# Eight weight buffers instead of six, x^T at two places in its tiles, early side loads on the main queue

## The chip, the cores and the metric

The kernel runs on one core of a Trainium2 chip, in one launch. The metric is device microseconds (us) of that core. The parts of the core that matter are TensorE (matrix products, PE in the rows; its weight loads are listed apart as PEld), VectorE (DVE), ScalarE (ACT), GpSimd (POOL) and SyncE (SP). SP computes nothing here: its sequence issues the loads, and an issue whose buffer is not free yet waits there with all that stand behind it. GpSimd's sequence issues loads too, among its own small operations.

## The reference

Two layers over 512 tokens of width 1024, in fp32. Layer 0 mixes the tokens by retention (4 heads), layer 1 by dilated sliding-window attention (3 groups of 16 heads, with a relative-position bias); behind each mixer stands a SwiGLU FFN of inner width 2816, and each of the four parts ends in a residual sum and a layer norm.

```
for i in range(2):
    mix = retention(x, w_in, w_out) if i == 0 else dilated_attention(x, w_in, w_out, rel_bias)
    x = layer_norm(1.414 * x + mix, gain[i, 0], bias[i, 0])
    gate, up = split(x @ w_up[i])
    x = layer_norm(1.414 * x + (silu(gate) * up) @ w_down[i], gain[i, 1], bias[i, 1])
```

In the retention, per head, the scores are q k^T times a decay table, y is the scores times v, normalised per token, and z = silu(gate) * y is multiplied by the output weights. In the attention the exponentials of the three groups share one maximum, are summed, divided once, and go through the output weights.

## The kernel before, in words

**Numbers.** Every fp32 operand of a large product is split into two parts, hi and lo, of a rounder fp32 type, and a product is three matmuls into the same accumulator, hi hi, hi lo, lo hi (`mm3`, line 278). In a trace row of a matmul the operand that moves is named first and the stationary one (brought by a weight load) second: in `bank<-xhi,whi 128x512` 512 columns of x^T move over 128 x 128 of a weight. x^T lies in `xhi` and `xlo` as 8 tiles of 128 features by 512 tokens. In the gates and in the q and k projections x^T moves over weights; in v, in the down projections (h) and in the output projections (z) the weights move over x^T, h or z.

**Weights.** All weights come in units of 128 x 1024 floats (512 KB), in an order fixed in advance (`plan`). A unit is loaded into one of six raw buffers (`wraw`, lines 66 to 80, on SP), split on ScalarE (`whi`, line 133) and on VectorE (`wlo`, line 134), two units ahead of its use. `load` issues the next load when the unit six places before it has been read by its last reader (lines 68 and 69). The first four units are loaded in halves, with the pieces of x^T between them.

**FFN.** The up projection goes through quads: four weight blocks n to n+3 against four quarters of x^T, in seven products instead of eight. The seven parts of a quad, each 24 matmuls of 256 columns, are in order block n, block n+1, a difference (n minus a sum), T1 against n+2, and so on (`up_rest`, line 773); the moving operands are quarters of x^T or combinations of them (T1 to T4). Three of the seven weight operands are sums of blocks, made on VectorE (`make_sum`, line 97, the instructions of line 107). The first of them needs n+2 plus n+3: block n+3 is loaded a second time, by GpSimd, and added into the raw buffer of n+2 in the transfer itself (`add_blocks`, line 89). A part that adds into a bank that has been in use waits until ScalarE has copied the bank (`copied`, line 739). Quads come in chunks of 4, 4 and 3; behind each chunk stand its down projections (8, 8 and 6 units, each 24 matmuls of 512 columns). In the first chunk of each FFN the work is mixed with the layer norm's last steps; the four later ones follow one pattern.

**Placement in SBUF.** Pools are laid out one behind the other in the order of their opening: constants, x^T and the residual, the raw buffers, a pad of 80 floats, the split weights, a small pool for statistics, and then the pools of the stage (retention, FFN, attention).

**Start.** SP first loads weights and x^T, then cosines, sines and the following units. GpSimd's sequence loads the columns for the layer norm (`cols`), the bias table and its one-hot matrices (`rbT`, `onehot`, both into the residual's tiles `r`, which are free then) and the decay tables (`dec`). TensorE uses the one-hot matrices in `bias_rows`, between the projections of q, k and v of the first head; the result is written to memory (`rows_dram`), from where GpSimd loads bias tables (`tab`, lines 882 and 889) for each pair of heads in the attention. For the powers in the norms GpSimd has one small operation per block of tokens (`rstd`, line 324: `grs` in the retention, `rs` in the layer norms).

Of the kernel before, what the change touches and what calls it, by code (L numbers as in the profile page):

```python
# [7 lines left out]
F32 = mybir.dt.float32  # L8
F32R = mybir.dt.float32r
# [6 lines left out]
P = 128  # L16
D = 1024
T = 512
KT = D // P
# [5 lines left out]
HD = 64  # L25
# [10 lines left out]
W0, W1, W2 = (2 * RES - 1) * PH, 256, 256  # L36
WB = W0 + W1 + W2
S0 = 7 * P


class Weights:
# [107 lines left out]
def trunk(tc, a, out):  # L149
    nc = tc.nc  # L150
    plan = []

    def ret_plan(h):
        qk = [(a["w_rqk"], 4 * h + i) for i in range(4)]
        v = [(a["w_rv"], 4 * h + i) for i in range(4)]
        g = [(a["w_rg"], 4 * h + i) for i in range(4)]
        o = [(a["w_ro"], 4 * h + i) for i in range(4)]
        return qk, v, g, o

    def ffn_plan(i):  # L160
        q = 0
        for n in FC:
            todo = [(q + k, j) for k in range(n) for j in range(7)]
            if q == 0:
                todo.sort(key=lambda t: (t[1] if t[0] < 2 and t[1] < 2 else 2))
                todo[4:9] = [(0, j) for j in (5, 3, 2, 6, 4)]
            plan.extend((a[f"w_up{i}"], 4 * k, j) for k, j in todo)
            plan.extend((a[f"w_dn{i}"], 2 * q + j) for j in range(2 * n))
            q += n

    rp = [ret_plan(h) for h in range(RH)]
    plan += rp[0][0] + rp[0][1]
    for h in range(RH):
        plan += rp[h][2]
        if h + 1 < RH:
            plan += rp[h + 1][0] + rp[h + 1][1]
        plan += rp[h][3]
    ffn_plan(0)
    tiles = {
        "qk": lambda p, i: [(a["w_aqk"], 6 * p + i)],  # L180
        "v": lambda q, g: [(a["w_av"], 6 * q + 2 * g + i) for i in range(2 + 2 * g)],
        "o": lambda q, _: [(a["w_ao"], 2 * q + i) for i in range(2)],
    }
    first, steps = att_schedule()
    for kind, *at in first + [s for t in steps for s in t]:
        if kind in tiles:
            plan += tiles[kind](*at)
    plan += tiles["o"](3, 0)
    ffn_plan(1)

    with tc.tile_pool(name="const", bufs=1) as cpool, tc.tile_pool(
        name="xpool", bufs=1
    ) as xpool, tc.tile_pool(name="wraw", bufs=6) as wraw, tc.tile_pool(
        name="pad", bufs=1
    ) as pad, tc.tile_pool(name="whl", bufs=4) as whl, tc.tile_pool(name="lnp", bufs=2) as lnp, tc.tile_pool(
        name="ps", bufs=8, space=PSUM
    ) as ps, tc.tile_pool(name="scratch", bufs=1, space=DRAM) as dr:
        pad.tile([P, 80], F32, name="pad")
        ws = Weights(nc, plan, wraw, whl, 2, 6)
        c = Core(nc, tc, a, out, ws, cpool, xpool, lnp, ps, dr)  # L200
        c.retention()
        c.ffn(0)
        c.attention(first, steps)
        c.ffn(1)
# [43 lines left out]
class Core:  # L248
    def __init__(self, nc, tc, a, out, ws, cpool, xpool, lnp, ps, dr):
        self.nc, self.tc, self.a, self.out, self.ws = nc, tc, a, out, ws  # L250
        self.lnp, self.ps, self.dr = lnp, ps, dr
        self.xhi = xpool.tile([P, KT, T], F32R, name="xhi")
        self.xlo = xpool.tile([P, KT, T], F32R, name="xlo")
        self.xw = [xpool.tile([P, 2, T], F32, name=f"xw{i}") for i in range(2)]
        self.r = [xpool.tile([P, D], F32, name=f"r{b}") for b in range(NB)]
        self.ident = cpool.tile([P, P], F32, name="ident")
        make_identity(nc, self.ident)
        self.mhalf = cpool.tile([P, 1], F32, name="mhalf")
        nc.vector.memset(self.mhalf, -0.5)
        self.cols = cpool.tile([P, 2, 2, KT], F32, name="cols")  # L260
        nc.gpsimd.dma_start(out=self.cols, in_=a["ln_cols"])
        self.on_read = False
        self.pending = []
        self.halves = False

    def bank(self):
        return self.ps.tile([P, T], F32, name="bank")
# [64 lines left out]
    def next_halves(self, i):  # L332


        self.halves, self.of = True, i

    def finish(self, b):
        for t, op in ((self.gain, ALU.mult), (self.bias, ALU.add)):
# [163 lines left out]
    def retention(self):  # L502
        nc, tc, a = self.nc, self.tc, self.a
        with tc.tile_pool(name="rt", bufs=1) as rt:
            self.rt = rt
            self.cos = rt.tile([P, T], F32, name="cos")
            self.sin = rt.tile([P, T], F32, name="sin")
            self.warm_up(rt)
            self.load_x(rt)
            nc.sync.dma_start(out=self.cos, in_=a["cos"])  # L510
            nc.sync.dma_start(out=self.sin, in_=a["sin"])
            qk = self.ret_qk()
            self.bias_rows()
            v = self.ret_v()
            for b in range(NB):
                nc.sync.dma_start(out=self.r[b], in_=a["x"][b * P : (b + 1) * P, :])
            self.next_halves(0)
            for h in range(RH):
                s = self.ret_scores(h, qk)
                g = [None] * 4  # L520
                last = h == RH - 1
                if not last:
                    for e in range(4):
                        g[e] = self.ret_gate(e)
                    y = self.ret_y(s, v)
                    qk = self.ret_qk()
                    tr = self.ret_transpose(y)
                    z = self.ret_z(g, tr)
                    v = self.ret_v()
                    self.rows_product(z, h == 0, False)  # L530
                else:
                    for e in range(2):
                        g[e] = self.ret_gate(e)
                    y = self.ret_y(s, v)
                    g[2] = self.ret_gate(2)
                    tr = self.ret_transpose(y)
                    g[3] = self.ret_gate(3)
                    z = self.ret_z(g, tr)
                    self.rows_product(z, False, True)

    def warm_up(self, rt):
# [78 lines left out]
    def ret_scores(self, h, qk):  # L620
        nc, rt = self.nc, self.rt
        dec = rt.tile([P, T], F32, name="dec", bufs=2)
        nc.gpsimd.dma_start(out=dec, in_=self.a["decay"][h])
        q, k = qk
        s = []
        for J in range(NB):
            n = T - J * P
            bk = self.bank()
            for d in range(2):
                self.mm3(  # L630
                    bk[:, :n],
                    (k[d][0][:, J * P : (J + 1) * P], k[d][1][:, J * P : (J + 1) * P]),
                    (q[d][0][:, J * P :], q[d][1][:, J * P :]),
                    d == 0,
                    d == 1,
                )
            t = rt.tile([P, T], F32, name="stmp", bufs=2)
            nc.vector.tensor_tensor(out=t[:, :n], in0=bk[:, :n], in1=dec[:, :n], op=ALU.mult)
            hi = rt.tile([P, n], F32R, name=f"s{J}hi")
            lo = rt.tile([P, n], F32R, name=f"s{J}lo")  # L640
            self.split(hi, lo, t[:, :n])
            s.append((hi, lo))
        return s
# [52 lines left out]
    def ffn(self, i):  # L696
        nc, tc = self.nc, self.tc
        with tc.tile_pool(name=f"ff{i}", bufs=1) as ff:
# [5 lines left out]
            self.xs = {"B11": self.x_block(0, 0), "B21": self.x_block(1, 0), "B22": self.x_block(1, 1)}  # L704
            self.xs["T1"] = self.x_block(0, 1)
            self.x_late = {}
            for n in ("T2", "T3", "T4"):
                self.xs[n] = [ff.tile([P, 4, T // 2], F32R, name=f"{n}{p}") for p in ("hi", "lo")]
            for ch, n in enumerate(FC):
                if ch == 1:  # L710
                    self.ln_params(2 * i + 1, *params)
# [6 lines left out]
                zs = [(hi[:, j, :], lo[:, j, :]) for hi, lo in quads for j in range(2)]  # L718
                last = ch == len(FC) - 1
                self.halves = False  # L720
                self.rows_product(zs, ch == 0, last, final=last and i == 1, finish=ch == 0)
    def part(self, bank, x, start=False):

# [97 lines left out]
    def attention(self, first, steps):  # L821
        nc, tc = self.nc, self.tc
        with tc.tile_pool(name="at", bufs=1) as at:
# [3 lines left out]
            self.vt += [at.tile([P, 12, P], F32, name=f"v{i}") for i in (1, 2)]  # L827
            self.ones = at.tile([P, P], F32R, name="ones")
            nc.vector.memset(self.ones.bitcast(F32), 1.0)
            self.half = at.tile([P, HD], F32, name="half")  # L830
            nc.vector.memset(self.half, 1.0)
            self.qt, self.kt = (
                [[at.tile([P, T], F32R, name=f"{w}{i}{n}") for n in ("hi", "lo")] for i in range(NG)]
                for w in "qk"
# [2 lines left out]
            n = 4  # L837
# [10 lines left out]
    def bias_rows(self):  # L848

        nc = self.nc  # L850
# [1 line left out]
        oh1 = self.r[2][0:33, 0 : W1 + W2]  # L852
        rows0, rows1 = self.r[1][0:AH, 0:W0], self.r[0][0:AH, 0 : W1 + W2]
        nc.gpsimd.memset(rb[32:33, :], NEG)
        nc.gpsimd.dma_start(out=rb[0:32, :], in_=self.a["rbT"])
        nc.gpsimd.dma_start(out=oh0, in_=self.a["onehot"][:, 0:W0])
        nc.gpsimd.dma_start(out=oh1, in_=self.a["onehot"][:, W0:WB])
        half = W0 // 2
        parts = [(0, oh0[:, :half], rows0[:, :half]), (0, oh0[:, half:], rows0[:, half:])]
        parts += [(1, oh1[:, :W1], rows1[:, :W1]), (2, oh1[:, W1:], rows1[:, W1:])]  # L860
# [220 lines left out]
    def att_pv(self, p, _):  # L1081
# [23 lines left out]
                lambda t: t[:, 2 * J * P : 2 * J * P + n], False, J == 3,  # L1105
            )
        for h in range(2):
            self.mm(den[h * HD : (h + 1) * HD], self.half, e[:, h], True, True)
        self.pv = bk, den, e

    def att_norm(self, p, _):
# [136 lines left out]
```

## Time and profile before

| what | us |
|---|---|
| median of 3 runs (lowest to highest) | 1703.7 (1700.6 to 1705.23) |
| the profiled execution | 1714.11 |
| its span, first to last instruction | 1712.3 |
| TensorE busy | 1654.3 (97%) |
| VectorE busy | 1067.7 (62%) |
| ScalarE busy | 648.4 (38%) |
| GpSimd busy | 220.5 (13%) |

The mean granted clock of TensorE is 0.982 of full speed over the span. Busy times say how long an engine had an instruction in work, and a matmul at a lower clock is busy for longer; a long busy time is thus not the same as much work. The windows below give both: the busy time of a stretch and, in the column PEclk, the clock in it.

### The profile page before, as it was taken

What the parts mean: (1) busy time and instruction counts of PE and PEld (TensorE: products, weight loads), DVE (VectorE), ACT (ScalarE), POOL (GpSimd) and SP (SyncE); (2) the same over time, 40 slices, a digit from 0 to 9 for tenths busy, and PEclk for the clock granted to TensorE, in tenths of its full rate; (3) what the DMA queues carried; (4) which work ended last, traced back from release to release, by engine and by line L of the source; (5) the groups of instructions that cost most, each with busy time, mean ns of one, the idle gap of its engine ahead of it and who ended that gap; (6) DMA issues with size and microseconds to landing.
All of it is one profiled execution on the core that took longest, in us unless ns stands there. A gap on an engine that the chain in (4) does not pass through costs nothing. (4 is left out here: it accounts for less than half of the span.)

```text
span 1712.3 us, 24333 instructions
## 1 busy us (share of the span) xinstructions
PE 1654.3 (97%) x9972; PEld 1432.7 (84%) x9972; DVE 1067.7 (62%) x1391; ACT 648.4 (38%) x937; POOL 220.5 (13%) x307
## 2 busy tenths in 40 slices
PE   9999999999899899899999999999999899989997
PEld 6888888888898898899878788788877898888896
DVE  6454454647994674657265574567569995575565
ACT  4322232325652451444332332333233752443351
POOL 0000000000000000006232332233311000000002
PEclk9999999999999999899999999999999999999999
DMA  7322223222453433433232223223321444334321
GB/s 276 129 71 96 74 72 101 87 74 79 126 166 106 115 114 94 114 111 100 98 95 79 86 87 87 87 76 97 88 74 50 117 130 148 99 112 134 90 84 50
DMA packets 52896, 174.33 MB, mean 102 GB/s; under 512 B 7764, under 2 KB 9828, under 8 KB 52784
## 3 DMA queue, kind: packets, MB, share of 16 engines
q1 hardware_dynamic: 44272, 155.81, 27.1%
q0 software_dynamic: 8512, 16.97, 5.6%
q8 instruction: 78, 1.28, 0.3%
q14 instruction: 34, 0.28, 0.1%
HBM read 170.57 MB, written 2.17 MB: 101 GB/s over the span
## 5 line engine op out<-in xcount | busy, mean ns | idle before, releaser
L134 DVE TENSOR_TENSOR wlo<-wraw,whi 128x1024 fp32r<-128x1024 f32 (+1 forms) x278 | 339.8, 1228 | 361.2 <-ACT whi L133 360.1
L133 ACT ACTIVATE whi<-wraw 128x1024 fp32r<-128x1024 f32 (+1 forms) x278 | 292.7, 1055 | 675.3 <-PE bank L270 357.7
L270 PE MATMUL bank<-xhi,whi 128*128 128x256 f32 (+1 forms) x1376 | 459.4, 334 | 9.1 <-ACT xhi L275 8.4
L270 PE MATMUL bank<-xhi,wlo 128*128 128x256 f32 (+1 forms) x1376 | 456.3, 332 | 3.6 <-DVE wlo L134 3.6
L270 PE MATMUL bank<-xlo,whi 128*128 128x256 f32 (+1 forms) x1376 | 455.8, 331 | 1.5 <-DVE xlo L276 1.5
L270 PEld LDWEIGHTS bank<-xhi,whi 128*128 128x128 f32 x1376 | 261.3, 190 | 40.2 <-ACT xhi L275 11.4
L270 PEld LDWEIGHTS bank<-xhi,wlo 128*128 128x128 f32 x1376 | 261.4, 190 | 32.5 <-DVE wlo L134 4.8
L270 PEld LDWEIGHTS bank<-xlo,whi 128*128 128x128 f32 x1376 | 261.6, 190 | 28.3 <-DVE xlo L276 2.1
L270 PE MATMUL bank<-whi,hlo 128*128 128x512 f32 x352 | 138.7, 394 | 0.0
L270 PE MATMUL bank<-wlo,hhi 128*128 128x512 f32 x352 | 138.0, 392 | 0.0
L270 PE MATMUL bank<-whi,hhi 128*128 128x512 f32 x352 | 136.8, 389 | 0.0
L882 POOL DMA_DIRECT2D tab<-rows_dram x128 | 69.5, 552 | 198.5 <-DVE s L1006 196.1
L133 ACT ACTIVATE whi<-sum 128x1024 fp32r<-128x1024 f32 x66 | 70.1, 1063 | 62.6 <-PE bank L270 51.9
L89 POOL DMA_DIRECT2D wraw<-in_w_up_dram x22 | 19.1, 869 | 559.3 <-DMA wraw<-in_w_up_dram 276.0
L454 DVE TENSOR_TENSOR r<-r,bank 128x512 f32<-128x512 f32 x78 | 52.3, 683 | 57.3 <-PE bank L270 57.3
L270 PE MATMUL bank<-whi,xlo 128*128 128x512 f32 (+1 forms) x256 | 86.0, 336 | 0.0
L270 PE MATMUL bank<-whi,xhi 128*128 128x512 f32 (+1 forms) x256 | 86.0, 336 | 0.0
L270 PE MATMUL bank<-wlo,xhi 128*128 128x512 f32 (+1 forms) x256 | 85.7, 335 | 0.0
L134 DVE TENSOR_TENSOR wlo<-sum,whi 128x1024 fp32r<-128x1024 f32 x66 | 80.4, 1220 | 8.1 <-ACT whi L133 8.1
L270 PE MATMUL bank<-T3hi,whi 128*128 128x256 f32 x176 | 57.8, 328 | 25.6 <-ACT tmp L739 25.6
L270 PEld LDWEIGHTS bank<-wlo,hhi 128*128 128x128 f32 x352 | 66.1, 188 | 15.1
L270 PEld LDWEIGHTS bank<-whi,hhi 128*128 128x128 f32 x352 | 66.1, 188 | 14.4
(279 smaller groups left out, 3006.2 us busy)
## 6 DMA issues: line engine op xcount, KB each, us to landing
wraw<-in_w_up_dram SPq DMA_DIRECT2D x88, 512.0 KB, 3.6
wraw<-in_w_aqk_dram SPq DMA_DIRECT2D x48, 512.0 KB, 3.5
wraw<-in_w_dn_dram SPq DMA_DIRECT2D x44, 512.0 KB, 3.6
wraw<-in_w_av_dram SPq DMA_DIRECT2D x24, 512.0 KB, 3.5
wraw<-in_w_up_dram POOLq DMA_DIRECT2D x22, 512.0 KB, 6.5
wraw<-in_w_rv_dram SPq DMA_DIRECT2D x16, 512.0 KB, 4.2
wraw<-in_w_rg_dram SPq DMA_DIRECT2D x16, 512.0 KB, 4.9
wraw<-in_w_ro_dram SPq DMA_DIRECT2D x16, 512.0 KB, 3.5
```

The lines of the kernel that those rows point to most:

```text
L89: self.nc.gpsimd.dma_start(out=self.raw_tiles[u], in_=a[n + 3], accum_op=ALU.add)
L133: self.nc.scalar.activation(hi[:, c], src[:, c], AF.Copy)
L134: self.nc.vector.tensor_tensor(out=lo[:, c], in0=src[:, c], in1=hi[:, c].bitcast(F32), op=ALU.subtract)
L270: self.nc.tensor.matmul(out=out, lhsT=lhsT, rhs=rhs, start=start, stop=stop, skip_group_check=self.on_read)
L454: nc.vector.tensor_tensor(out=dst, in0=dst, in1=bk, op=ALU.add)
L882: self.nc.gpsimd.dma_start(out=tab[r * RUN : (r + 1) * RUN, h, b * P : (b + 1) * P].rearrange("p (r l) -> p r l", r=RES), in_=src(h * WB + ...
```

## The change

The raw buffers become eight (`bufs` of the pool and of `Weights`). The room comes from the memory that the kernel sets aside for the descriptors of GpSimd's transfers, `dynamic_dma_scratch_size`, which is now 8192 bytes per partition, and from one small tile of ones that another now serves for. The pool for statistics stands first behind the constants, and the pad ahead of the split weights is gone. The x^T tiles are 128 columns longer; x^T lies at their start, and from a layer norm ahead of an FFN until that FFN's down projections it lies 48 floats further (`place_x`). T2 to T4 are put behind a pad of 48 floats in the FFN's pool, with a pad of 80 behind them. The loads of `cols`, `rbT`, `onehot` and of the first two decay tables are issued on SP. The mark from which GpSimd's accumulating loads for the first FFN may be issued (`next_halves(0)`, which sets `of`) stands ahead of the last output product instead of ahead of the heads.

```diff
+SHIFT = 48
@@ trunk @@
-    ) as xpool, tc.tile_pool(name="wraw", bufs=6) as wraw, tc.tile_pool(
-        name="pad", bufs=1
-    ) as pad, tc.tile_pool(name="whl", bufs=4) as whl, tc.tile_pool(name="lnp", bufs=2) as lnp, tc.tile_pool(
+        name="lnp", bufs=2
+    ) as lnp, tc.tile_pool(name="xpool", bufs=1) as xpool, tc.tile_pool(
+        name="wraw", bufs=8
+    ) as wraw, tc.tile_pool(name="whl", bufs=4) as whl, tc.tile_pool(
-        pad.tile([P, 80], F32, name="pad")
-        ws = Weights(nc, plan, wraw, whl, 2, 6)
+        ws = Weights(nc, plan, wraw, whl, 2, 8)
@@ Core @@
-        self.xhi = xpool.tile([P, KT, T], F32R, name="xhi")
-        self.xlo = xpool.tile([P, KT, T], F32R, name="xlo")
+        self.xt = [xpool.tile([P, KT * T + P], F32R, name=n) for n in ("xhi", "xlo")]
+        self.place_x(0)
-        nc.gpsimd.dma_start(out=self.cols, in_=a["ln_cols"])
+    def place_x(self, shift):
+        self.xhi, self.xlo = [
+            t[:, shift : shift + KT * T].rearrange("p (k t) -> p k t", t=T) for t in self.xt
+        ]
@@ next_halves @@
         self.halves, self.of = True, i
+        self.place_x(SHIFT)
@@ retention @@
+            nc.sync.dma_start(out=self.cols, in_=a["ln_cols"])
-            self.next_halves(0)
...
                     z = self.ret_z(g, tr)
+                    self.next_halves(0)
                     self.rows_product(z, False, True)
@@ ret_scores @@
-        nc.gpsimd.dma_start(out=dec, in_=self.a["decay"][h])
+        (nc.sync if h < 2 else nc.gpsimd).dma_start(out=dec, in_=self.a["decay"][h])
@@ ffn @@
+            ff.tile([P, SHIFT], F32, name="pad")
             for n in ("T2", "T3", "T4"):
                 self.xs[n] = [ff.tile([P, 4, T // 2], F32R, name=f"{n}{p}") for p in ("hi", "lo")]
+            ff.tile([P, P - SHIFT], F32, name="pad2")
...
                 self.halves = False
+                self.place_x(0)
@@ attention @@
-            self.half = at.tile([P, HD], F32, name="half")
-            nc.vector.memset(self.half, 1.0)
...
-            self.mm(den[h * HD : (h + 1) * HD], self.half, e[:, h], True, True)
+            self.mm(den[h * HD : (h + 1) * HD], self.ones[:, 0:HD].bitcast(F32), e[:, h], True, True)
@@ bias_rows: rbT and the two parts of onehot @@
-        nc.gpsimd.dma_start(...)
+        nc.sync.dma_start(...)
@@ kernel @@
-    nc = bacc.Bacc("TRN2", target_bir_lowering=False, num_devices=1)
+    nc = bacc.Bacc("TRN2", target_bir_lowering=False, num_devices=1, dynamic_dma_scratch_size=8192)
```

Three places show what moves. The rows are instructions in the order of an engine's sequence, with the line in that kernel; `x4` stands for four of a kind in a row, and the numbers behind `r` are those of tiles.

SP at the start, before, from the cosines on: `w_rv`, `w_rg` and `w_rqk` are weight units, `x` the residual.

```order
L510 DMA cos<-in_cos_dram 128x512
L511 DMA sin<-in_sin_dram 128x512
L77 DMA wraw<-in_w_rv_dram 128x1024 x4
L77 DMA wraw<-in_w_rg_dram 128x1024 x4
L77 DMA wraw<-in_w_rqk_dram 128x1024
L516 DMA r_85<-in_x_dram 128x1024
L516 DMA r_86<-in_x_dram 128x1024
L867 DMA rows_dram<-r_84 16x672
L868 DMA rows_dram<-r_83 16x512
L77 DMA wraw<-in_w_rqk_dram 128x1024 x2
```

The same place with the change.

```order
L517 DMA cos<-in_cos_dram 128x512
L518 DMA sin<-in_sin_dram 128x512
L519 DMA cols<-in_ln_cols_dram 128x32
L78 DMA wraw<-in_w_rv_dram 128x1024 x4
L78 DMA wraw<-in_w_rg_dram 128x1024 x4
L78 DMA wraw<-in_w_rqk_dram 128x1024 x2
L864 DMA r_82<-in_rbT_dram 32x48
L865 DMA r_82<-in_onehot_dram 33x672
L866 DMA r_81<-in_onehot_dram 33x512
L78 DMA wraw<-in_w_rqk_dram 128x1024
L631 DMA dec<-in_decay_dram 128x512
L78 DMA wraw<-in_w_rqk_dram 128x1024
```

The side loads have come in: `cols` ahead of the weight units, `rbT` and `onehot` behind the tenth of these units, the decay tables behind the next two, and the residual's loads have gone behind the two writes of bias rows.

SP where the first FFN's weights begin, before: `w_up` and `w_dn` are the units of the up and down projections, `gain` and `bias` the layer norm's rows.

```order
L77 DMA wraw<-in_w_up_dram 128x1024 x6
L329 DMA gain<-in_ln_gain_dram 128x1024
L330 DMA bias<-in_ln_bias_dram 128x1024
L77 DMA wraw<-in_w_up_dram 128x1024 x10
L77 DMA wraw<-in_w_dn_dram 128x1024 x5
L329 DMA gain<-in_ln_gain_dram 128x1024
L77 DMA wraw<-in_w_dn_dram 128x1024 x2
L330 DMA bias<-in_ln_bias_dram 128x1024
L77 DMA wraw<-in_w_dn_dram 128x1024
L77 DMA wraw<-in_w_up_dram 128x1024 x16
```

And with the change.

```order
L78 DMA wraw<-in_w_up_dram 128x1024 x8
L335 DMA gain<-in_ln_gain_dram 128x1024
L336 DMA bias<-in_ln_bias_dram 128x1024
L78 DMA wraw<-in_w_up_dram 128x1024 x8
L78 DMA wraw<-in_w_dn_dram 128x1024 x7
L335 DMA gain<-in_ln_gain_dram 128x1024
L78 DMA wraw<-in_w_dn_dram 128x1024
L78 DMA wraw<-in_w_up_dram 128x1024
L336 DMA bias<-in_ln_bias_dram 128x1024
L78 DMA wraw<-in_w_up_dram 128x1024 x15
```

The loads of weights stand up to two units further ahead of all else in this sequence, as eight buffers let them.

GpSimd from the start to the first FFN, before: `dec` is a decay table, `grs` the powers of the retention's norm (four per head), `rs` those of the layer norm, and L89 is the accumulating load.

```order
L854 MEMSET r_86 1x48
L855 DMA r_86<-in_rbT_dram 32x48
L856 DMA r_86<-in_onehot_dram 33x672
L857 DMA r_85<-in_onehot_dram 33x512
L623 DMA dec<-in_decay_dram 128x512 x3
L324 TENSOR_TENSOR grs<-veps,mhalf 128x1 x4
L623 DMA dec<-in_decay_dram 128x512
L324 TENSOR_TENSOR grs<-veps,mhalf 128x1 x12
L89 DMA wraw<-in_w_up_dram 128x1024
L324 TENSOR_TENSOR rs<-veps,mhalf 128x1 x4
L89 DMA wraw<-in_w_up_dram 128x1024 x10
```

And with the change, where L90 is that load.

```order
L863 MEMSET r_82 1x48
masks.py:199 ISA
masks.py:199 AFFINE_SELECT ident<-ident 128x128
L631 DMA dec<-in_decay_dram 128x512
L330 TENSOR_TENSOR grs<-veps,mhalf 128x1 x4
L631 DMA dec<-in_decay_dram 128x512
L330 TENSOR_TENSOR grs<-veps,mhalf 128x1 x8
L90 DMA wraw<-in_w_up_dram 128x1024
L330 TENSOR_TENSOR grs<-veps,mhalf 128x1 x4
L90 DMA wraw<-in_w_up_dram 128x1024
L330 TENSOR_TENSOR rs<-veps,mhalf 128x1 x4
L90 DMA wraw<-in_w_up_dram 128x1024 x9
```

The early loads are gone from here, and the first accumulating load stands ahead of the last four `grs` instead of behind them. TensorE's and ScalarE's sequences are the same as before, VectorE's but for a few neighbours.

## Rows read from the trace of the kernel before

**Rows 1.** The page's head and its busy times by engine.

```profile
span 1712.3 us, 24333 instructions
...
PE 1654.3 (97%) x9972; PEld 1432.7 (84%) x9972; DVE 1067.7 (62%) x1391; ACT 648.4 (38%) x937; POOL 220.5 (13%) x307
```

**Rows 2.** Waits: engine, tile, line, released by: total us, times, longest us.

```profile
POOL tab L882 <- DVE s L1006: 196.1, 7, 33.2
...
DVE sum L107 <- DMA wraw<-in_w_up_dram: 61.6, 14, 5.7
...
PE bank L270 <- ACT tmp L739: 27.4, 12, 3.8
```

**Rows 3.** Windows of the four later up stages, the first and their sum (us, busy).

```profile
548.60:638.20 89.60, 82.71 (x674) 81.89 (x673) 61.00 (x65) 44.41 (x58) 2.58 (x3) 0.94 0.42 123
...
sum 317.50, PE 289.72 PEld 286.81 DVE 212.01 ACT 154.94 POOL 8.60; mean PE 72.43 PEld 71.70 DVE 53.00 ACT 38.74 POOL 2.15
```

**Rows 4.** Windows: two quads without waits, and 270 us of the retention.

```profile
467.50:486.60 19.10, 19.10 (x171) 19.10 (x170) 19.10 (x21) 11.87 (x16) 0.86 (x1) 1.00 0.52 152
619.10:638.20 19.10, 19.10 (x171) 19.10 (x171) 12.93 (x15) 11.46 (x15) 0.00 (x0) 1.00 0.34 112
...
100.00:370.00 270.00, 270.00 (x1220) 222.09 (x1219) 142.57 (x208) 76.58 (x100) 4.98 (x9) 1.00 0.26 85
```

**Rows 5.** Timeline, a quad's third block: start, duration, engine, work [wait <-releaser].

```profile
550.65 1.22 DVE L134 TENSOR_TENSOR wlo<-wraw,whi 128x1024 fp32r<-128x1024 f32 x1
563.08 2.35 DVE L134 TENSOR_TENSOR wlo<-wraw,whi 128x1024 fp32r<-128x1024 f32 x2
565.46 0.33 SPq L77 DMA_DIRECT2D wraw<-in_w_up_dram  x1
570.84 0.86 POOL L89 DMA_DIRECT2D wraw<-in_w_up_dram  x1 [18.91 <-DMA wraw<-in_w_up_dram]
577.48 1.23 DVE L107 TENSOR_TENSOR sum<-wraw 128x1024 f32<-128x1024 f32 x1 [4.57 <-DMA wraw<-in_w_up_dram]
586.18 0.58 PE L270 MATMUL bank<-T3hi,whi 128*128 128x256 f32 x1 [2.30 <-ACT tmp L739]
```

**Rows 6.** Windows behind a wait of TensorE: at half clock, then at full.

```profile
562.20:565.60 3.40, 3.40 (x18) 3.40 (x17) 3.23 (x3) 1.08 (x2) 0.00 (x0) 0.50 0.11 11
565.70:569.00 3.30, 3.30 (x30) 3.30 (x30) 1.41 (x2) 1.55 (x2) 0.00 (x0) 1.00 0.74 284
```

**Rows 7.** Timeline of TensorE: ends of three runs of equal matmuls.

```profile
81.21 0.39 PE L270 MATMUL bank<-v1hi,s1hi 128*128 128x512 f32 x1
86.42 0.39 PE L270 MATMUL bank<-v3hi,s3lo 128*128 128x512 f32 x1
87.82 0.39 PE L270 MATMUL bank<-xhi,wlo 128*128 128x512 f32 x1
107.42 0.39 PE L270 MATMUL bank<-xhi,wlo 128*128 128x512 f32 x1
638.18 0.39 PE L270 MATMUL bank<-whi,hhi 128*128 128x512 f32 x1
682.13 0.28 PE L270 MATMUL bank<-xhi,whi 128*128 128x256 f32 x1
```

**Rows 8.** Timeline at the start: splits of v's units, and the one-hot product.

```profile
22.22 1.23 DVE L134 TENSOR_TENSOR wlo<-wraw,whi 128x1024 fp32r<-128x1024 f32 x1 [1.50 <-ACT whi L133]
29.41 1.30 PE L270 MATMUL bank<-r 33*16 33x336 f32 x4
```

**Rows 9.** Timeline ahead of the first FFN: a split, the last head's first power.

```profile
367.59 1.23 DVE L134 TENSOR_TENSOR wlo<-wraw,whi 128x1024 fp32r<-128x1024 f32 x1 [3.68 <-ACT whi L133]
375.67 0.55 POOL L324 TENSOR_TENSOR grs<-veps,mhalf 128x1 f32<-128x1 f32 x1 [83.44 <-DVE veps L323]
```

**Rows 10.** The page's DMA issues: count, KB each, median us to landing.

```profile
wraw<-in_w_up_dram SPq DMA_DIRECT2D x88, 512.0 KB, 3.6
...
tab<-rows_dram POOLq DMA_DIRECT2D x128, 16.0 KB, 2.0
```

More of the change, by code (lines that the diff above doesn't have):

```diff
@@ L191, in trunk @@
     with tc.tile_pool(name="const", bufs=1) as cpool, tc.tile_pool(
-        name="xpool", bufs=1
-    ) as xpool, tc.tile_pool(name="wraw", bufs=6) as wraw, tc.tile_pool(
-        name="pad", bufs=1
-    ) as pad, tc.tile_pool(name="whl", bufs=4) as whl, tc.tile_pool(name="lnp", bufs=2) as lnp, tc.tile_pool(
+        name="lnp", bufs=2
+    ) as lnp, tc.tile_pool(name="xpool", bufs=1) as xpool, tc.tile_pool(
+        name="wraw", bufs=8
+    ) as wraw, tc.tile_pool(name="whl", bufs=4) as whl, tc.tile_pool(
         name="ps", bufs=8, space=PSUM
     ) as ps, tc.tile_pool(name="scratch", bufs=1, space=DRAM) as dr:
-        pad.tile([P, 80], F32, name="pad")
-        ws = Weights(nc, plan, wraw, whl, 2, 6)
+        ws = Weights(nc, plan, wraw, whl, 2, 8)
         c = Core(nc, tc, a, out, ws, cpool, xpool, lnp, ps, dr)
@@ L854, in bias_rows @@
         nc.gpsimd.memset(rb[32:33, :], NEG)
-        nc.gpsimd.dma_start(out=rb[0:32, :], in_=self.a["rbT"])
-        nc.gpsimd.dma_start(out=oh0, in_=self.a["onehot"][:, 0:W0])
-        nc.gpsimd.dma_start(out=oh1, in_=self.a["onehot"][:, W0:WB])
+        nc.sync.dma_start(out=rb[0:32, :], in_=self.a["rbT"])
+        nc.sync.dma_start(out=oh0, in_=self.a["onehot"][:, 0:W0])
+        nc.sync.dma_start(out=oh1, in_=self.a["onehot"][:, W0:WB])
         half = W0 // 2
```

## The prediction, made before the result was known

> **What bounds the kernel now.** I read the page first: TensorE is busy 97% of a span of 1712.3 us, VectorE 62%, ScalarE 38% [rows 1]. The order of TensorE's instructions does not change, so time can come only from matmuls that run closer together or from the moments in which TensorE waits. The list of waits, read next, has one such wait of weight that comes again and again: 27.4 us in 12 pieces on the copy of a bank (L739), beside 61.6 us in 14 pieces in which VectorE's subtraction of two weight blocks (L107) waits for a load of `w_up` [rows 2]. Fourteen is the number of quads in the four later up stages (4 and 3 in each FFN; a quad is 168 matmuls of 256 columns).
>
> The windows of these stages put a price on it. Together they take 317.5 us, of which TensorE is busy 289.72, and the granted clock is 0.94 in the first of them [rows 3]. A quad that waits for nothing takes 19.1 us at clock 1.00, even one in which VectorE is busy throughout [rows 4]. Fourteen such quads are 267.4 us; the stages therefore hold 50.1 us that is not matrix work at full clock. 27.4 of it is the wait; the rest is mostly the clock: behind each wait stands a stretch of 3.4 us (sometimes two) at 0.50, the 1.2 GHz level, in which 18 matmuls start where 30 start in the 3.3 us behind it [rows 6].
>
> The timeline of one quad shows what the wait hangs on [rows 5]. Its third block (n+2) can be loaded when a raw buffer comes free; with six buffers that is the one of block n of the quad before, whose last reader ends at 563.08 + 2.35 = 565.43. SP issues the load at 565.46; GpSimd adds block n+3 into it 5.4 us later (570.84), and VectorE's subtraction starts at 577.48, 6.6 us after that, having waited 4.57. Everything behind it on VectorE, ScalarE and so TensorE is late: at 586.18 TensorE has stood 2.30 us.
>
> **The change part by part.** *Eight raw buffers.* Units are loaded in the order n, n+1, n+2, n+3, four to a quad; with eight buffers n+2 takes the buffer of n+2 two quads back. Its last reader ends at 550.65 + 1.22 = 551.87 in the same quad [rows 5], 13.6 us before the present one. With the same 5.4 and 6.6 us behind it the block is there at about 564, and VectorE asks for it at 577.48 - 4.57 = 572.9: 8.9 us to spare. The first quads of a chunk take buffers of down-projection units, each of which lasts 24 matmuls of 512 columns, 5.5 us at the rate of [rows 7]; two units earlier are 11 us, also more than the longest wait of 5.7. So the fourteen waits go, the clock keeps its upper level as in [rows 4], and what is late next is VectorE: 212 us of work in stages of 267.4, 79%, which left TensorE unhurt in a quad where it was 100%. Gain: 50.1 us. The least I can defend is the bare wait, 27.4 us, if the clock falls for another reason; the most is 50.1.
>
> *Placement.* The order of the matmuls stays, but where their operands lie does not. In the kernel before, the 80-float pad puts the split weights 320 bytes further than x^T, modulo 512, and tiles made later (h, z) at x^T's offset. After it, the pad is gone, the small pool stands first, and all of x^T, weights, h, z, v, s are multiples of 512 bytes apart, except x^T and T2 to T4 in an FFN's up stages (48 floats, 192 bytes): there the distance is 320 as now. The trace has three rates for matmuls of 512 columns, start to start at clock 1.00 [rows 7]: x moving over weights, 84 steps from 87.82 to 107.42, 233.3 ns; weights moving over h, 192 steps from 638.18 to 682.13, 228.9 ns; v moving over s in the retention, already 512 apart, 23 steps from 81.21 to 86.42, 226.5 ns. By the program's counts x moves in 384 (gates) + 384 (retention q, k) + 1056 (attention q, k) = 1824 matmuls, and weights move in 1056 (h) + 576 (z) + 768 (v of both layers) = 2400. If all come to 226.5: 1824 x 6.8 = 12.4 us and 2400 x 2.4 = 5.8 us, together 18.2. The 576 attention matmuls of 256 columns that change their distance are unmeasured; a step of 2 ns would be 1 us, taken as nothing. Bounds: all the difference (18.2 gained), or, if v over s is quick for another reason and distance 0 costs what x pays now, 2400 x 4.4 = 10.6 us lost. I take 18.2, since it is the one row at that distance.
>
> The rates in [rows 7] differ with the pair of operands though shape and clock are the same. The Trainium skill says otherwise (SBUF — State Buffer, section "Who interferes with whom"): TensorE reads the moving operand and the weights through two independent ports and never waits on anyone there. By that rule placement gives nothing and the sum is the buffers alone; the trace does not bear it out as far as three pairs can say.
>
> *Early side loads.* `cols`, `rbT`, two `onehot` pieces and two `dec` go from GpSimd to SP. The dangerous ones are `rbT` and `onehot`: on SP they stand behind the 14th weight unit, whose buffer is released by the second split in the run that starts at 22.22 (1.23 each, [rows 8]), so they are issued at about 25 to 26, and with the 3.6 us that a weight load takes [rows 10], or a little more because they share the rings with two of them, they land at 29 to 30.5. TensorE wants them at 29.41 [rows 8]. Cost: between 0 and 3 us (1 of wait and a stretch at half clock); I take 1. `cols` is one more issue of some 0.4 us ahead of loads that have time; the first `dec` stands one weight unit further back, and its scores come only behind 384 matmuls of v.
>
> *GpSimd's order.* The first accumulating load now stands ahead of the last head's four `grs`. Its block follows the split that ends at 367.59 + 1.23 = 368.8, lands 4 to 5.4 us later, takes 0.9 to issue, and is off GpSimd at about 374 to 375; the first `grs` is at 375.67 [rows 9]. Nothing, or up to 1 us if it is late (the y of one block). `ones` for `half`, and the later mark for halves, issue the same instructions: nothing.
>
> *The smaller scratch* costs nothing as long as GpSimd does not have to wait for space to write descriptors; the trace shows no such wait, and cannot show one for half the size (a rival, below).
>
> **Sum.** On the profiled execution (1714.1 us): 1714.1 - 50.1 - 18.2 + 1 = 1646.8. That execution is 10.4 us above the median of the runs, and I do not know in which part; taking the same 67.3 off the median gives 1703.7 - 67.3 = 1636.4. If the 10.4 lie in the waits, the gain is that much smaller, 1647.
>
> **The rivals.**
> - *Placement is worth nothing* (the ports are independent, and the three rates have other reasons). For: only 23 steps stand for distance 0, and v and s are not x and weights. Against: x moving and weights moving are long rows, 4.4 ns apart, over the same tiles. Time: 1703.7 - 50.1 + 1 = 1655.
> - *The stalls stay.* VectorE or ScalarE, or the load after it (n of the next quad), takes the place of the late block. For: VectorE's order is almost untouched, and 79% is not little. Against: a quad with VectorE at 100% lost nothing [rows 4]. Time: 1703.7 - 18.2 + 1 = 1686.5.
> - *The clock does not stay up.* TensorE busy without a gap in longer stages might draw the lower level of itself. Against: 270 us of 100% busy at 1.00 [rows 4]. It would leave the 22.7 us: 1659.
> - *Slower: the halved scratch makes GpSimd's issues wait.* 16 table loads of 0.55 us each go out in a row per head pair (128 in all), and land after 2.0 us in the median [rows 10]. If each had to wait until the one before had landed, 16 x 2.55 + 2 x 4.3 = 49 us stand where 10.2 do now. GpSimd stands idle 196.1 us in 7 pieces ahead of these rows [rows 2], 28 us each; taking that as the slack of a table, the 39 us more exceed it by 11, seven times: 77 us, so 1636 + 77 = 1713. It decides from the point where only one table load fits into the scratch; with two in flight the extra wait is halved and stays within the slack. Against: these loads are 16 KB each, small beside the 512 KB accumulating loads that the same scratch carries.
> - *Nothing of it works* (the load of n+2 bound by something else, and placement nothing): 1704.
>
> **How the numbers follow.** Both terms about as worked out: 76%, 1636, and by itself 1624 to 1650. Placement nothing: 9% (1655). Clock: 3% (1659). Stalls stay: 6% (1686). GpSimd waits: 3% (1713). Nothing: 3%. A measurement of this kernel tells about 0.3%, 5 us, from no change. All but the last two cases are faster by more than that: 0.94; the last is the same, 0.03; slower 0.03. The range is 1622 to 1659: it holds the first case with its gain's unknown ends and the two next to it, and leaves out the rest.
>
> **What would show it.** Right: no wait of L107 for `w_up` in the later chunks, the wait of TensorE for L739 gone from the list, clock 1.00 and about 19.1 us per quad in the four stages, a span about 66 us shorter; x over weights at 226 to 227 ns start to start, h too; the first accumulating load off GpSimd before the last head's `grs`. Wrong: stages of more than 80 us for four quads, with VectorE named as the releaser; x over weights still at 233; TensorE waiting for `onehot` at 29 by more than 3 us; gaps between the 16 table issues. An up stage whose matmuls of 256 columns no longer keep 113 to 114 ns would show that the distance kept there was not the reason for that rate.

## The result

| | us |
|---|---|
| the change, median of 4 runs (lowest to highest) | 1660.82 (1656.48 to 1662.27) |
| the kernel before, median of 4 runs | 1702.15 (1700.13 to 1705.23) |
| ratio, with its 95% interval | 0.9751 [0.9726, 0.9777] |
| predicted | 1636, range 1622 to 1659 |

The change is faster by 41 us where 67 were forecast, and the time lies 2 us above the range. The direction and the mechanism of the largest part held; two prices did not, and a rate that was counted on was not there.

The page of the changed kernel, its head and its busy times, beside [rows 1]:

```profile
span 1654.7 us, 24316 instructions
...
PE 1626.4 (98%) x9972; PEld 1423.4 (86%) x9972; DVE 1068.1 (65%) x1390; ACT 650.7 (39%) x937; POOL 216.0 (13%) x301
```

The lines of its list of waits that answer to [rows 2]:

```profile
DVE sum L108 <- DMA wraw<-in_w_up_dram: 26.7, 4, 7.4
...
PE bank L276 <- DMA r<-in_rbT_dram: 3.4, 1, 3.4
...
PE bank L276 <- ACT tmp L750: 1.9, 2, 0.9
```

TensorE's wait for the copied bank has gone from 27.4 us to 1.9, and none of the four waits that VectorE has left lies in the four later up stages. In their place TensorE waits once for a side load. The windows of the four stages (the first, and the sum), with the columns of [rows 3]: the window and its length, the busy time and number of instructions of PE, PEld, DVE, ACT and POOL, the granted clock, the busy share of the DMA engines, and GB/s.

```profile
544.30:623.50 79.20, 79.20 (x674) 79.16 (x673) 61.62 (x65) 45.29 (x58) 1.69 (x2) 1.00 0.45 133
...
sum 277.20, PE 277.20 PEld 277.10 DVE 214.13 ACT 157.83 POOL 5.10; mean PE 69.30 PEld 69.27 DVE 53.53 ACT 39.46 POOL 1.28
```

TensorE is busy from end to end at clock 1.00, as forecast; and yet the stages take 277.2 us and not 267.4. A quad takes 19.8 us without waiting for anything. That is the first thing to explain. The timeline of TensorE over x^T and over h, where [rows 7] had 233.3 and 228.9 ns:

```profile
89.06 0.39 PE L276 MATMUL bank<-xhi,wlo 128*128 128x512 f32 x1
107.42 0.39 PE L276 MATMUL bank<-xhi,wlo 128*128 128x512 f32 x1
...
623.50 0.39 PE L276 MATMUL bank<-whi,hhi 128*128 128x512 f32 x1
667.02 0.28 PE L276 MATMUL bank<-xhi,whi 128*128 128x256 f32 x1
```

The first pair is 81 steps apart, 226.7 ns each; the second 192 steps, 226.7. Distance 0 gave x^T and h the rate that v over s had shown.

The start (SP and TensorE in the timeline), beside [rows 8]:

```profile
21.58 0.42 SPq L864 DMA_DIRECT2D r<-in_rbT_dram  x1
...
30.70 1.29 PE L276 MATMUL bank<-r 33*16 33x336 f32 x4 [3.44 <-DMA r<-in_rbT_dram]
```

And the windows behind that wait:

```profile
32.40:35.80 3.40, 3.40 (x10) 2.15 (x8) 3.40 (x6) 1.23 (x2) 0.00 (x0) 0.50 0.01 2
36.00:39.40 3.40, 3.40 (x16) 2.81 (x16) 1.65 (x5) 0.00 (x0) 0.00 (x0) 1.00 0.80 268
```

The load was issued earlier than I had thought and landed 9.0 us later, at 30.6; TensorE, faster over x^T and not held up for 1.56 us ahead of its first product with x^T as in the profile before, asked for it at 27.3. It waited 3.44 us, and a stretch at half clock followed.

GpSimd ahead of the first FFN, beside [rows 9], and the page's DMA issues beside [rows 10]:

```profile
370.36 0.93 POOL L90 DMA_DIRECT2D wraw<-in_w_up_dram  x1 [79.55 <-DMA wraw<-in_w_up_dram]
372.86 0.55 POOL L330 TENSOR_TENSOR grs<-veps,mhalf 128x1 f32<-128x1 f32 x1 [1.57 <-DVE gmv L670]
```

```profile
tab<-rows_dram POOLq DMA_DIRECT2D x128, 16.0 KB, 2.1
...
r<-in_rbT_dram SPq DMA_DIRECT2D x1, 6.0 KB, 9.0
```

The accumulating load is off GpSimd 1.57 us before the first power is asked for, and the table loads land as before: these two cost nothing.

### The profile page after: what moved, and what is told of

Its sections match the earlier page's. It is cut to its first block, busy times and chain, and to the rows that moved or that the text cites. A ratio compares the mean times of both kernels' runs of the same rounds, so it can differ in the third digit from the quotient of the medians.

```text
span 1654.7 us, 24316 instructions
## 1 busy us (share of the span) xinstructions
PE 1626.4 (98%) x9972; PEld 1423.4 (86%) x9972; DVE 1068.1 (65%) x1390; ACT 650.7 (39%) x937; POOL 216.0 (13%) x301
## 3 DMA queue, kind: packets, MB, share of 16 engines
q0 software_dynamic: 8192, 16.26, 5.8%
## 4 chain that ended last, share of the span: by engine, by line
PE 91%; DVE 5%; DMA 2%; issue 1%; ACT 1%; POOL 0%; SPq 0%; DVEq 0%; POOLq 0%; ACTq 0%
PE bank L276 90%; DVE wlo L135 2%; DVE sum L108 1%; DMA wraw<-in_w_rqk_dram 1%; DMA r<-in_rbT_dram 1%; PE bank L683 0%; PE bank L1036 0%; DVE r L461 0%; DMA wraw<-in_w_rv_dram 0%; ACT whi L134 0%; DVE st L351 0%; DVE xlo L282 0%; ACT xw L410 0%; PE bank L394 0%; POOL rs L330 0%
## 5 line engine op out<-in xcount | busy, mean ns | idle before, releaser
L90 POOL DMA_DIRECT2D wraw<-in_w_up_dram x22 | 18.9, 858 | 602.7 <-DMA wraw<-in_w_up_dram 322.2
L276 PEld LDWEIGHTS bank<-whi,hlo 128*128 128x128 f32 x352 | 66.1, 188 | 13.7
```

What stands on the lines that cost most here:

```text
L90: self.nc.gpsimd.dma_start(out=self.raw_tiles[u], in_=a[n + 3], accum_op=ALU.add)
L276: self.nc.tensor.matmul(out=out, lhsT=lhsT, rhs=rhs, start=start, stop=stop, skip_group_check=self.on_read)
```

## The experiments

All times are medians; ratios are to the kernel before on the same chip.

| | us | ratio [95%] | four later up stages, us |
|---|---|---|---|
| E1 kernel before, again | 1703.64 | 0.9994 [0.9980, 1.0008] | 307.1 |
| E2 eight buffers only | 1661.15 | 0.9743 [0.9727, 0.9758] | 266.5 |
| E3 placement and side loads only | 1688.19 | 0.9911 [0.9888, 0.9934] | 302.7 |
| E4 change, rbT and onehot on GpSimd | 1652.84 | 0.9696 [0.9674, 0.9719] | 277.0 |
| E5 as E4, h at distance 192 | 1646.67 | 0.9653 [0.9633, 0.9674] | 266.7 |
| E6 as E4, a short matmul at each stage's entry | 1645.20 | 0.9645 [0.9623, 0.9666] | 266.9 |
| E8 the change, again | 1660.94 | 0.9739 [0.9689, 0.9789] | 277.0 |
| E9 the change with E6's short matmul | 1651.29 | 0.9681 [0.9642, 0.9719] | 266.9 |
| E10 as E6, with 128 columns (one run) | 1651.98 | - | 277.2 |

My first theory after the result: matmuls of 256 columns at distance 320 have two rates, 113.3 and 117.8 ns, and a run keeps the one that it enters with until TensorE waits. The kernel before shows both in one stage (first and last of two runs with 80 and 104 steps):

```profile
549.33 0.28 PE L270 MATMUL bank<-xhi,whi 128*128 128x256 f32 x1
558.40 0.28 PE L270 MATMUL bank<-xhi,wlo 128*128 128x256 f32 x1
...
566.72 0.28 PE L270 MATMUL bank<-xhi,whi 128*128 128x256 f32 x1
578.97 0.28 PE L270 MATMUL bank<-T2hi,wlo 128*128 128x256 f32 x1
```

9.07 / 80 = 113.4 ns and 12.25 / 104 = 117.8 ns, both over parts of x^T and T2; between them lie a wait and a stretch at half clock. The rival to this theory: the new places of the tiles make the up stages slow.

**E1, the kernel before unchanged.**

> The kernel before, unchanged, to see what its undisturbed runs are made of (its profiled execution was 12 us above the median of its runs). Theory: the number of stretches at half clock differs from run to run, so the granted clock of the runs lies above the 0.982 of that profile, about 0.988, and the time at about 1702. Rival: the clock is 0.982 in these runs too, and the 12 us belong to something else.

The clock of its ten runs is 0.987 to 0.991, above the 0.982 of the first profile. Its waits and the sum of its four stages (546.1 to 635.3, 679.2 to 745.5, 1462.0 to 1549.8, 1593.8 to 1657.6):

```profile
DVE sum L107 <- DMA wraw<-in_w_up_dram: 62.0, 14, 6.2
PE bank L270 <- ACT tmp L739: 23.4, 12, 3.0
```

```profile
sum 307.10, PE 281.37 PEld 278.43 DVE 211.92 ACT 154.97 POOL 8.61; mean PE 70.34 PEld 69.61 DVE 52.98 ACT 38.74 POOL 2.15
```

The waits are all there, but fewer of them are followed by half clock: in the four stages 4 stretches, 17.1 us in all, where the first profile has 10 with 41.0 (over the whole execution, its end included, 7 with 31.1 and 14 with 63.3). The stages of this execution, which is 0.7 us below the median of its ten though its clock of 0.991 is their highest, hold 307.1 us and not 317.5. The rival that stands in this expectation falls.

The third of these stages shows something more. It is entered from down projections at 229.0 ns, and yet it runs at 117.8 up to its first wait (its first matmul, and the 73rd):

```profile
1462.01 0.28 PE L270 MATMUL bank<-xhi,whi 128*128 128x256 f32 x1
1470.49 0.28 PE L270 MATMUL bank<-xhi,whi 128*128 128x256 f32 x1
```

8.48 / 72 = 117.8 ns; the other three stages of E1 start at 113.3. The rate of what stands ahead is thus not the whole rule. In all, 762 of the matmuls of E1's four stages run at 117.8, which costs 3.4 us, against 162 in the first profile.

**E2, eight buffers and the smaller scratch on the kernel before.**

```diff
-    ) as xpool, tc.tile_pool(name="wraw", bufs=6) as wraw, tc.tile_pool(
+    ) as xpool, tc.tile_pool(name="wraw", bufs=8) as wraw, tc.tile_pool(
-        ws = Weights(nc, plan, wraw, whl, 2, 6)
+        ws = Weights(nc, plan, wraw, whl, 2, 8)
-    nc = bacc.Bacc("TRN2", target_bir_lowering=False, num_devices=1)
+    nc = bacc.Bacc("TRN2", target_bir_lowering=False, num_devices=1, dynamic_dma_scratch_size=8192)
```

> Only the eight raw buffers and the smaller scratch; placement and side loads as before. Theory of two rates (the 256-column matmuls at a distance of 320 run at 113.3 or at 117.8 ns, and whichever a stage is entered with is kept until TensorE waits): no waits in the four later up stages, their entry is at 113.3 as in the kernel before, so they keep 113.3: four quads 76.2 us, three 57.1; about 1660. Rival (the rate of 117.8 belongs to a stage without waits): four quads 79.2 us, about 1670. If GpSimd suffers from the smaller scratch, gaps between the table issues.

```profile
549.00:625.20 76.20, 76.20 (x673) 76.16 (x672) 60.87 (x65) 45.37 (x58) 1.72 (x2) 1.00 0.46 137
...
sum 266.50, PE 266.50 PEld 266.46 DVE 211.37 ACT 158.10 POOL 5.16; mean PE 66.62 PEld 66.61 DVE 52.84 ACT 39.52 POOL 1.29
```

76.2 us for four quads: 113.4 ns without any wait. So a stage without waits is not slow of itself. This part alone is as fast as the whole change. VectorE is busy 79% of these stages and holds nothing up.

**E3, the change with six buffers.** In the changed kernel `bufs=8` and the `8` of `Weights` become 6; the smaller scratch stays.

> The changed kernel with six raw buffers again: placement and side loads alone. Both theories: 512-column matmuls at 226 to 227 ns, some 16 us; the start about 4 us slower; the waits in the up stages stay: about 1690. Theory of two rates: the 256-column matmuls of the later up stages show 113.3 behind some of the waits and 117.8 elsewhere, both in one stage. Rival (the new places of the tiles make them slow): 117.8 throughout.

In the first of its stages the runs go 117.8, 113.3 behind the first wait, then 117.8: both rates with the new placement, and the rival of the new places falls. All steps of one kind summed against E1's trace, 512 columns at full clock: x^T over weights 1730 steps from 233.3 to 227.2 ns (10.5 us), weights over h 1048 from 228.9 to 226.8 (2.3), the other 1314 or so 3.8 us; together 16.6. The 576 of 256 columns in the attention went from 118.0 to 120.4, 1.4 us the other way.

**E4, rbT and onehot back on GpSimd.**

```diff
-        nc.sync.dma_start(out=rb[0:32, :], in_=self.a["rbT"])
+        nc.gpsimd.dma_start(out=rb[0:32, :], in_=self.a["rbT"])
```

and the same for the two pieces of onehot.

> The changed kernel with rbT and onehot on GpSimd again, all else as changed. If the wait of 3.8 us and the half clock behind it at the start come from these loads being late on SP, both go: some 4 to 5 us faster than the changed kernel, about 1656. Rival: the wait is taken over by the weight loads that then follow sooner: no change, 1661.

TensorE goes into the one-hot product without a wait:

```profile
27.19 1.02 PE L276 MATMUL bank<-r 33*16 33x336 f32 x3
```

By 52 us the kernel is 5.0 us ahead of the profiled execution of the change, and stays so into the first FFN: the wait of 3.44 and the half clock. The medians are 8.1 apart, and the trace of E8, the changed kernel once more, shows where the rest can lie: its wait is a little longer, and the half clock around it lasts 10.2 us instead of 3.4.

```profile
31.47 2.40 PE L276 MATMUL bank<-r 33*16 33x336 f32 x4 [4.14 <-DMA r<-in_onehot_dram]
```

```profile
29.40:39.60 10.20, 8.13 (x18) 4.25 (x19) 8.31 (x15) 1.59 (x3) 0.00 (x0) 0.50 0.47 150
```

At 52 us E8 is 8.1 us behind E4. E9 has the same long stretch, and the profiled execution of the change is the fastest of its four, so 8 us is as well supported as 5 (E9 and E6, the same pair with the short matmul, are 6.1 apart). The lateness needs the eight buffers too: in E3, with six, eight weight units stand ahead of rbT on SP instead of ten, it lands 5.8 us after its issue, and TensorE enters the one-hot product at 30.05 without a wait. In both it lands 0.2 us behind the unit ahead of it.

**E5, h at the old distance.** The pad of 48 floats goes ahead of the tiles of h instead of T2 to T4, which puts both behind it.

```diff
+            ff.tile([P, SHIFT], F32, name="pad")
             ff.tile([P, 2, T], F32, name="hhi", bufs=FC[0])
...
-            ff.tile([P, SHIFT], F32, name="pad")
             for n in ("T2", "T3", "T4"):
...
+            ff.tile([P, 2, T], F32, name="hlo", bufs=FC[0])
             ff.tile([P, P - SHIFT], F32, name="pad2")
```

> The previous experiment's kernel (the change, with rbT and onehot on GpSimd; 1652.8 us), but with the tiles of h 192 bytes off the weights, as in the kernel before. Theory of two rates, set by what a stage is entered from: the down projections run at 228.9 ns again (2.4 us lost over 1056 matmuls, a little more if they take their slow form), the later up stages are entered from that rate and stay at 113.3 ns: 2352 x 4.5 = 10.6 us gained; about 1645. Rival (in a kernel with the new placement the up stages run at 117.8 ns of themselves): only the loss, 1655.

**E6, a short matmul.** At the entry of each later up stage:

```diff
+        if self.kick:
+            self.mm(bank[:, 0:64], hi[:, 0:P], xh[:, 0, 0:64], True, True)
+            self.kick = False
```

> The same base with one matmul of 64 columns more at the entry of each of the four later up stages, into the bank that the next matmul starts anew. Theory of two rates: the step from one rate to the other depends on how the two streams stand to each other at the entry, so the short matmul can move a stage to 113.3 ns (up to 10.6 us, about 1643), or leave it at 117.8 if it comes out the same way (1653). Rival: 117.8 in any case, 1653.

The first of the four stages in E5, and in E6:

```profile
538.80:615.00 76.20, 76.20 (x673) 76.16 (x672) 60.92 (x65) 45.32 (x58) 1.72 (x2) 1.00 0.45 137
```

```profile
540.70:617.00 76.30, 76.30 (x674) 76.29 (x673) 60.93 (x65) 45.31 (x58) 1.72 (x2) 1.00 0.46 137
```

Both bring the stages from 79.2 to 76.2 or 76.3, with the placement of x^T and T as in the change. What precedes a stage decides its rate, though not by its own rate alone (the third stage of E1). E6 and E5, at 1645.2 and 1646.7, are not told apart by their intervals; they are the fastest versions, and beat both kernels.

**E7, TensorE alone.**

> TensorE alone, none of the kernel's work (the output is zeros): the three-matmul pattern over constant tiles at distances 0, 32, ... 480 bytes between weights and moving operand: runs of 36 matmuls of 512 columns, and runs of 72 to 96 of 256 columns, entered from 512-column runs at distance 0, at distance 192, and behind a wait. Theory: the rate depends on the distance with nothing else running; at 512 columns distance 0 gives about 226.7, 192 about 229 and 320 about 233; at 256 columns and distance 320 it is 117.8 when entered from distance 0 and 113.3 when entered from distance 192, and either behind a wait. Rival (the two rates come from the other engines' traffic): one rate for all entries and distances.

With none of the kernel's work running the rate still depends on the distance, and at 512 columns it repeats every 256 bytes (start to start, the last 30 steps of a run): 226.7 to 227.4 at distances 0 (in the entry runs; the very first run begins with steps of 427 ns) and 256; 228.9 at 192 and 448; 232.3 to 234.3 at all others, 320 among them. Two of the sixteen entry runs at 192 took 233.3, so this rate has a history as well. At 256 columns: 117.8 or 113.3 at 64, 192 and 448, by what stood ahead, 117.8 at 320, 116.7 to 120.0 at the rest. Two runs of 72 steps at distance 448, the first entered from distance 0 and the second from 192 (their first matmul, and the first behind them):

```profile
390.02 0.28 PE L62 MATMUL bank<-xhi,whi 128*128 128x256 f32 x1
398.50 0.40 PE L62 MATMUL bank<-xhi,whi 128*128 128x512 f32 x1
...
658.42 0.28 PE L62 MATMUL bank<-xhi,whi 128*128 128x256 f32 x1
666.58 0.39 PE L62 MATMUL bank<-xhi,whi 128*128 128x512 f32 x1
```

8.48 / 72 = 117.8 ns and 8.16 / 72 = 113.3. But at 320 I had expected 113.3 behind an entry from 192, and it was 117.8 behind all three entries: the entry decides, but not by the simple rule that I had written, and E7 did not bring out 113.3 at the distance of the kernel's up stages.

**E8 and E9, the change beside the change with E6's short matmul**, the edit as in E6.

> The changed kernel itself, beside the next one on the same chip: 1661, the four later up stages 79.15 and 59.36 us, the start with a wait of about 3.5 us for rbT or onehot.

> The changed kernel with nothing but the short matmul at the entry of the four later up stages. If the two causes (rate of the up stages, late side loads) add: 267 us instead of 277 in the four stages, so 9 to 10 us faster than the changed kernel, about 1652; with the side loads on GpSimd it was 1645. Rival (the earlier gain of the short matmul was chance between chips): no difference.

9.7 us between the medians, 10 in the four stages: the cause stands by itself, and adds to that of the side loads.

**E10, the short matmul with 128 columns.**

> The kernel with side loads on GpSimd and a short matmul of 128 columns instead of 64. If what counts is how the two operand streams stand to each other at the entry, another length may leave a stage at 117.8 (79.2 us); if any interruption of the pattern clears it, 113.3 (76.3 us). No sure side: I take 113.3 at six in ten.

```profile
538.60:617.80 79.20, 79.20 (x675) 79.20 (x673) 61.61 (x65) 45.35 (x58) 1.72 (x2) 1.00 0.44 132
```

79.2: no help, against my guess. An interruption of the pattern alone does not clear the slow rate: in this one execution all four stages kept it. That agrees with two streams (the moving operand and the weights) that lock in one of two relations, but no run here looks at the relation itself: why there are two rates stays open.

## Why the prediction failed, step by step

| term | predicted gain | measured | where |
|---|---|---|---|
| waits and clock in the four stages | 50.1 | 40.6 | 307.1 in E1, 266.5 in E2 |
| rate of the up stages | 0 | -10.7 | 277.2 in the change, 266.5 in E2 |
| placement, 512 columns | 18.2 | 16.6 | E3 against E1 |
| placement, 256 columns in the attention | 0 | -1.4 | E3 against E1 |
| side loads at the start | -1 | -5.0 | E4 against the profiled execution of the change (-8.1 against E8) |
| sum | 67.3 | 40.1 | 41.3 between the medians |

With the side loads at 8.1 the sum is 37.0: 1 to 4 us of the gain belong to no row, and the close fit of 40.1 is in part luck. The first row also holds the 3.4 us that E1 lost by the slow rate.

**Eight buffers: the mechanism was right.** The chain of [rows 5] is gone with them, the clock stays up, VectorE at 77% (79% in E2) does not take over, and E2 shows the stages within a microsecond of the 267.4 worked out.

**The step that failed first** is the price of a quad: "the clock keeps its upper level as in [rows 4]", and with it 19.1 us for each of fourteen. The clock did keep its level; the price did not hold, 19.8. Both quads of [rows 4] stand behind a wait, in a run that had come out of it at 113.3 ns. In the change nothing waits, the stages are entered from down projections at 226.7 ns, and all 2352 matmuls run at 117.8. The prediction put the effect of a new placement on these stages at nothing, since x^T kept its distance there; but the placement of h, counted as 2.5 us of gain, took 10 away next door (277.0 in E4, 266.7 in E5). My text named the sign ("an up stage whose matmuls of 256 columns no longer keep 113 to 114 ns"), but not as a case with a price.

**The step that failed second** is "taking the same 67.3 off the median". The 10.4 us by which the profiled execution stood above the median lay in the very term that I took from it: the four stages are 10.4 us longer in that execution than in E1, with 41.0 us at half clock against 17.1. I had named this, and the 1647 that follows from it, and still gave the other number.

**Placement, 512 columns:** right, 16.6 for 18.2, since x^T came to 227.2 on the mean and not 226.5. The rival by which placement is worth nothing fell; the Trainium skill's rule behind it (SBUF — State Buffer, section "Who interferes with whom": independent ports, no waiting), by which placement would give nothing, does not agree with E7, where TensorE alone runs at 226.7 or 233.3 ns by the distance of its two operands.

**Side loads:** the right place, the wrong size: 5 to 8 us for 1. 3.6 us to landing was a median over the whole kernel; at the start SP had issued ten weight units ahead in the same queue, the last of them landed at 30.4, and rbT took 9.0. The prediction had named this as a sign of being wrong (a wait there of more than 3 us).

**GpSimd's order, the smaller scratch:** nothing, as forecast. The 16 table loads take 8.7 us as before.

**The rivals:** none came true; what came was a case that none of them held. That 1660.8 lies near the 1659 of the clock's rival is chance: the clock in the stages was 1.00.

## What to carry to other kernels

A stretch chosen as the undisturbed reference has a history: look at what stood ahead of it, and whether other undisturbed stretches run at the same rate. Before a term is taken off a median, ask whether the profiled execution is a usual one in just that term; here more than half of the time at half clock in the four stages was this execution's own (41.0 us against 17.1). And a wait can change the rate of what follows it (E3): after it is gone, check the rate of what runs through, start to start.

## What was not expected of the hardware

- Matmuls of one shape over the same tiles have two steady rates, 113.3 and 117.8 ns at 256 columns; each lasts for hundreds of matmuls (672 in one stage), and a matmul of 64 columns at the entry changed it where one of 128 did not.
- With TensorE alone, a 512-column matmul takes 226.7 to 234.3 ns depending on the distance between its moving operand and the weights, with a period of 256 bytes.
- The same waits are not always followed by half clock: in the same four stages 10 stretches in one execution, 4 in another of the same kernel.
- A load of 6 KB behind ten of 512 KB in one queue, at least three of them landed before it was issued, landed after 9.0 us, 0.2 us behind the last of them.
